# First block of a streaming encoder step: scaling out of PSUM, another place for the fourth tile, fills inside the turns' banks, a pinned order

## The chip, the cores and the metric

The kernel runs on one core of one Trainium2 chip. The core has five engines, each with a queue of its own that is worked off in order: TensorE (PE in the profile, its weight loads PEld), VectorE (DVE), ScalarE (ACT), GpSimd (POOL) and SyncE (SP), which here only issues DMA transfers. They meet through semaphores. SBUF is the working memory; PSUM, eight banks of 128 x 512 fp32, is what PE writes into. The metric is the device time of one launch in microseconds (us), lower is better; several runs are given by their median.

## The reference

One layer of an encoder trunk on 2048 prompt frames and 32 sample frames of 1024 features:

```
hn   = rmsnorm(h, g_mix)
proj = hn @ w_in                       # six parts of 512 columns: h, b, c, za, v, zb
yA   = b * conv3(c * h) * silu(za)     # causal convolution of width 3
yB   = poolmix(v) * silu(zb)           # trailing means of 2/4/8/16 frames, a map per group
h    = h + concat(yA, yB) @ w_out
h    = h + (p @ w_ple) * sigmoid(rmsnorm(h, g_ple) @ w_ple_gate)
y    = rmsnorm(h, g_final)
```

Beside y, the last rows of the convolution's and the pooling's inputs are returned. All is fp32. `rmsnorm` divides a row by the root of its mean square and multiplies it by a vector g along the features.

## The kernel before

Products are made in split form: a factor is cast to a short high part on ACT (line 78), the rest is a low part, got by a subtraction on DVE (line 79), and three products (high by high, high by low, low by high) give one in fp32. The helper `split` issues both; `put` (line 349) does it into a tile's two halves.

The 2080 frames are five blocks of 416. The first two blocks are one group, and its first unit (128 columns of each of the six parts) is done plainly, part after part; the other units use a scheme with seven products for eight. This change lies in what comes before and in that first unit, the first 76 us or so.

Block 0 is fetched as three tiles of 128 frames and a fourth with the last 32 frames of block 0 and the last 32 of block 1 (`ahead0`, `short0`, lines 610 and 611). For each tile ACT sums squares (line 89), POOL makes the mean and, by a power of -1/2, the factor of the row (lines 70 and 74), DVE scales the tile by that factor and by g in two halves of 512 features (`normal`, line 405), PE turns each half into a PSUM bank by four transposes (`turn`, line 412), and `put` splits the bank into `B0`. The vector g reaches all 128 rows through a product with a row of ones into two banks (line 376); DVE copies them to `g_bc` in SBUF (line 377).

PSUM has two rings: `bank` hands out six banks, `tbank` two. A ring hands out a bank once everything that reads its last content is over. Eight turns go through the six; the two of the fourth tile take the banks of the first tile's two. A further bank of the small ring, `idle`, takes transposes of the identity matrix whose result nobody reads, issued by `keep_busy` between the turns (line 615): 8 ahead of the first, then 1, 1, 1, 12, 1, 1, 3 and 2 after the turns.

Then three weights (zb, v, c) are split in halves (`weights`, line 520), and the unit begins with the high-by-high products of the three parts (`upper_parts`, line 585, `zb_first`, `v_first`, `c_first`, 8 products each, line 582). Their low parts follow, and between them PE turns block 1 (`second_block`, line 640: the fourth tile's 32 frames first, then its three tiles), turns a few vectors into a small-ring bank (`vectors`, line 692, `pv`) and goes on with the products of block 1 (`project`, line 570, whose products are on line 565) and the pooling's map (`mix`, line 755, `pm`).

What order an engine gets is decided before the launch by a planner, which goes by the order of the program and by estimated durations. `tc.keep_in_program_order(ins)` pins an instruction: those so marked keep their order among themselves on their engine. Before the change, the fills, the turns, the scalings and the frames' casts of the first block are pinned; the weights' casts, the products of `project` and `mix` aren't.

Of the kernel before, what the change touches and what calls it, by code (L numbers as in the profile page):

```python
# [12 lines left out]
ALU = mybir.AluOpType  # L13
PSUM = bass.MemoryType.PSUM

P = 128
D = 1024
# [7 lines left out]
NB = 416  # L25
GROUPS = [[0, 1], [2, 3], [4]]
NT = SEQ // P + 1
NH = D // 2
KH = KC // 2
# [6 lines left out]
def trunk(ctx, tc, x_p, x_s, c_conv, c_pool, p_p, p_s, g_mix, w_in, conv_w, conv_b, pool_w,  # L36
          pool_scale, w_out, g_ple, w_gate, w_ple, g_fin, y_p, y_s, sc_p, sp_p, sc_s, sp_s):
    nc = tc.nc
# [14 lines left out]
    def bank(name):  # L53
        return ps_m.tile([P, 512], F32, tag="mm", name=name)

    def tbank(name):
        return ps_t.tile([P, 512], F32, tag="tr", name=name)

    ident = const.tile([P, P], F32, name="ident")
# [17 lines left out]
    def split(hi, lo, src, eng=nc.vector):  # L77
        ins = nc.scalar.copy(hi, src)  # L78
        eng.tensor_tensor(lo, src, hi.bitcast(F32), op=ALU.subtract)
        return ins  # L80
# [3 lines left out]
    g_bc = const.tile([P, D], F32, name="g_bc")  # L84
# [223 lines left out]
    def ring4(t, name):  # L308
        return t.tile([P, D], F32, tag="t", name=name)
# [21 lines left out]
    with ExitStack() as s1:  # L331
# [14 lines left out]
        def wtile(name):  # L346
            return wr.tile([P, KH, 2, P], F32R, tag="w", name=name)

        def put(piece, src):

            return split(piece[:, :, 0], piece[:, :, 1], src)

        def ftile(name):
            return wk.tile([P, KH, P], F32, tag="f", bufs=4, name=name)
# [15 lines left out]
        nc.sync.dma_start(gm_row, g_mix)  # L370
        ones = ftile("ones").rearrange("p k n -> p (k n)")[:1, :P]
        nc.vector.memset(ones, 1.0)
        for half in range(2):
            cs = slice(half * NH, half * NH + NH)
            pg = tbank(f"gm_{half}")
            nc.tensor.matmul(pg, ones, gm_row[:, cs], start=True, stop=True)
            nc.vector.tensor_copy(g_bc[:, cs], pg)


        hn = {}  # L380
# [21 lines left out]
        def x_tile(name, rows, squares=junk):  # L402
            return x_stat(x_load(name, rows), squares=squares)

        def normal(x, later=False, cs=slice(0, D)):
            xt, n, r = x
            ins = nc.vector.scalar_tensor_tensor(xt[:n, cs], xt[:n, cs], r[:n], g_bc[:n, cs], op0=ALU.mult,
                                                 op1=ALU.mult)
            if later:
                tc.keep_in_program_order(ins)  # L410

        def turn(x, half, name, get=tbank, later=False):
            xt, n, _ = x
            pt = get(name)
            for k in range(KH):
                kk = half * KH + k
                ins = nc.tensor.transpose(pt[:, k * P:k * P + n], xt[:n, kk * P:(kk + 1) * P], ident[:n, :n])
                if later:
                    tc.keep_in_program_order(ins)
            return pt.rearrange("p (k t) -> p k t", k=KH)[:, :, :n]  # L420
# [91 lines left out]
        def raw_weight(kind, j, name, ring=raw_ring):  # L512
            t = ring(f"raw_{name}")
            col = cols[kind] * WA + j * P
            nc.sync.dma_start(t, w_in[:, col:col + P].rearrange("(k p) n -> p k n", p=P))
            return t
# [3 lines left out]
        def weights(kind, j, name):  # L520

            if first_w:
                return first_w.pop(0)
            raw = raw_weight(kind, j, name, lambda name: raw_of.pop(kind) if kind in raw_of else raw_ring(name))
            out = []
            for half in range(2):
                out.append(wtile(f"w_{name}_{half}"))
                put(out[-1], raw[:, half * KH:half * KH + KH])
            return out

        def pair_weights(gi, ka, kb, j, name, ring, s_ring):
# [26 lines left out]

            return make

        def half_product(ps, lhs, b, start, stop=True):

            for k in range(KH):
                for q, (x, y) in enumerate(((0, 0), (0, 1), (1, 0))):
                    nc.tensor.matmul(ps[:, :NB], lhs[:, k, x], b[:, k, y], start=start and k + q == 0,  # L565
                                     stop=stop and k == KH - 1 and q == 2, skip_group_check=True)

        begun = {}

        def project(ps, w, tb, between=None):  # L570
            x = hn[tb]
            for half in range(2):
                half_product(ps, w[half], x[half], half == 0, half == 1)
                if between and not half:
                    between()

# [8 lines left out]
        def upper_parts(kind, w, tb):  # L585

            ps = bank(f"{kind}_first")
            for half in range(2):
                part_of(ps, w, tb, half, 0, 0, start=half == 0)
            begun[kind] = ps  # L590
# [12 lines left out]
        B0 = {}  # L603
# [6 lines left out]
        ahead0 = [x_tile(f"0_{c}", [x_rows(0, c)], in_raw(kind)) for c, kind in enumerate(raw_of)]  # L610
        short0 = x_tile("0_3", [x_rows(0, 3), x_rows(1, 3)])
        B0.update(six(0))
        idle = tbank("idle")

        def keep_busy(n):

            for _ in range(n):
                tc.keep_in_program_order(nc.tensor.transpose(idle[:, :P], ident, ident))

        keep_busy(8)  # L620
        for x in (*ahead0, short0):
            for half in range(2):
                normal(x, True, slice(half * NH, half * NH + NH))
        for c, x in enumerate([*ahead0, short0]):
            n = P if c < 3 else DEC
            for half, q in enumerate(("11", "21")):
                ins = put(B0[q][:, :, :, c * P:c * P + n], turn(x, half, f"pt0_{c}_{half}", bank, True)[:, :, :n])
                tc.keep_in_program_order(ins)
                keep_busy(((1, 1), (1, 12), (1, 1), (3, 2))[c][half])
        hn[0] = B0["11"], B0["21"]  # L630
        ahead1 = []
        made = []
# [7 lines left out]
        def second_block():  # L640

            spans = [(c, slice(c * P, min(NB, c * P + P))) for c in range(4)]
            xs = [(x_stat(x, True), slice(0, P)) for x in ahead1]
            for x, _ in xs:
                normal(x, True)
            xs.append((short0, slice(DEC, 2 * DEC)))
            yield
            both = {}
            for c, cs in [spans[3], *spans[:3]]:
                x, ts = xs[c]  # L650
                n = ts.stop - ts.start
                both[c] = [x[0][:, half * NH:half * NH + KH * n].rearrange("p (k t) -> p k t", k=KH)
                           for half in range(2)]
                for half, q in enumerate(("12", "22")):
                    pt = turn(x, half, f"pt1_{c}_{half}", bank, later=True)[:, :, ts]
                    put(B0[q][:, :, :, cs], pt)
                    nc.scalar.copy(both[c][half], pt)
                yield
            op = lambda o, a, b, op=ALU.subtract: nc.vector.tensor_tensor(o, a, b, op=op)
            for c, cs in spans:  # L660
                p12, p22 = both[c]
                n = cs.stop - cs.start
                t1, t3, t2, t4 = (ftile(f"f{t}_1_{c}")[:, :, :n] for t in range(4))
                part = lambda q, h: B0[q][:, :, h, cs].bitcast(F32)
                op(t1, p12, part("11", 0))
                op(t3, p22, p12)
                op(t1, t1, part("11", 1))
                op(t2, p22, t1)
                put(B0["T2"][:, :, :, cs], t2)
# [12 lines left out]
        pw = one.tile([P, 2, 4, P], F32R, name="pw")  # L682
# [27 lines left out]
        class Unit:  # L710
# [44 lines left out]
            def mix(self, b):  # L755

                pp, j = self.cols(self.pooled.rearrange("p h n -> p (h n)"), b), self.j
                pq = self.pooled[:, 1, b * NB:b * NB + NB]
                pm = tbank(f"pm_{self.tag}_{b}")
                nc.tensor.matmul(pm[:, :NB], pw[:, 0, j], pp, start=True, stop=False)  # L760
                nc.tensor.matmul(pm[:, :NB], pw[:, 0, j], pq, start=False, stop=False)
                nc.tensor.matmul(pm[:, :NB], pw[:, 1, j], pp, start=False, stop=True)
                z = self.cols(self.zs, b)
                nc.vector.scalar_tensor_tensor(z, pm[:, :NB], pscale(j), z, op0=ALU.mult, op1=ALU.mult)
                self.store(4 + j, b, self.zs)
# [451 lines left out]
    with ExitStack() as s2:  # L1217
# [112 lines left out]
        for i in range(0, NT - 1, 2):  # L1330
            with tc.issue_after(loaded[-1].ins):
                x = [load_rows(xh, "x", i + b, x_p) for b in range(2)] if i else [first_x, second_x]
# [4 lines left out]
            if last:  # L1337
                n = tiles[NT - 1][1]
# [6 lines left out]
            if last:  # L1345
                x = load_rows(xh, "x", NT - 1, x_p, x_s)
# [27 lines left out]
        _, run = embed(rest_e, wp, ring)  # L1374
# [6 lines left out]
        for k in range(KH):  # L1381
            raw = [ring4(xh, f"wg_r{k}_{i}") for i in range(2)]
# [265 lines left out]
        n = tiles[NT - 1][1]  # L1648
# [62 lines left out]
```

## Time and profile before

| | |
|---|---|
| time, median of 3 runs | 921.82 us (920.5 to 921.92) |
| the profiled execution's own time | 921.55 us |
| its span, first to last instruction | 919.8 us |
| PE busy | 907.4 us (99%) |
| DVE, ACT, POOL busy | 723.6, 478.9, 153.6 us |
| DMA | 186.37 MB, mean 203 GB/s |

A row of the profile gives a start and a duration in us from the span's start, the engine, the line of the kernel (L407 is line 407), the operation, what it writes and reads with buffer numbers left out, the shape and, after x, how many were merged into the row. In brackets stands the idle time in front of it and what ended that. PE's durations contain a tail in which the next matmul already runs, so the pace of a run of matmuls is read from the starts. The chain of waits is followed back from the last instruction, at each step to what released it.

### The profile page before, as it was taken

How to read it: one execution, taken by the hardware profiler on the slowest of the kernel's cores; microseconds unless marked ns; L12 is line 12 of the kernel's file. 1: busy time of each engine (PE TensorE's matmuls, PEld its weight loads, DVE VectorE, ACT ScalarE, POOL GpSimd, SP SyncE). 2: the span in 40 equal slices, each digit the busy share in tenths (PEclk: the TensorE clock that was granted, in tenths of full speed). 3: DMA queues.
4: the chain of work that ended last, by engine and by line, in shares of the span. 5: the costliest groups of instructions: out<-in, count | busy, mean ns of one | idle time of the engine just before them, and what ended most of it. 6: DMA issues, size and time to landing. Idle time of an engine off the chain costs nothing.

```text
span 919.8 us, 13006 instructions
## 1 busy us (share of the span) xinstructions
PE 907.4 (99%) x4515; PEld 821.9 (89%) x4515; DVE 723.6 (79%) x1235; ACT 478.9 (52%) x883; POOL 153.6 (17%) x271
## 2 busy tenths in 40 slices
PE   8999999999999999999999999999999999999996
PEld 7999999999999999999999987888877868878885
DVE  6996989999488989785778679665554798888875
ACT  7744565554345555443545446344334875465555
POOL 4111322212001111000000011111111002323333
PEclk9999999999999999999999999999999999999999
DMA  8255595769935555457765359756775885799892
GB/s 261 79 156 151 162 274 157 210 201 314 414 114 162 181 160 187 118 178 264 203 177 170 125 192 295 254 190 184 252 216 170 307 263 146 185 222 241 205 264 101
DMA packets 140734, 186.37 MB, mean 203 GB/s; under 512 B 12060, under 2 KB 111260, under 8 KB 139389
## 3 DMA queue, kind: packets, MB, share of 16 engines
q1 hardware_dynamic: 120237, 126.33, 45.1%
q0 software_dynamic: 17696, 53.71, 20.0%
q10 hardware_dynamic: 2736, 5.51, 1.8%
q8 instruction: 35, 0.57, 0.3%
q14 instruction: 30, 0.25, 0.1%
HBM read 128.93 MB, written 56.56 MB: 202 GB/s over the span
## 4 chain that ended last, share of the span: by engine, by line
PE 89%; DVE 4%; DMA 3%; ACT 1%; issue 1%; SPq 0%; POOL 0%; DVEq 0%; ACTq 0%; POOLq 0%
PE x_o L168 9%; PE x_zbv L565 7%; PE x_ch L565 7%; PE x_zab L565 7%; PE x_g L168 6%; PE e L103 5%; PE z_o L168 4%; PE z_zbv L565 3%; PE z_ch L565 3%; PE z_zab L565 3%; PE b L565 3%; PE za L565 3%; PE h L565 3%; PE z_g L168 3%; PE v L565 2%; PE c L565 2%
## 5 line engine op out<-in xcount | busy, mean ns | idle before, releaser
L103 PE MATMUL e<-wq,pps 128*128 128x512 f32 (+1 forms) x156 | 38.9, 399 | 0.2 <-ACT pps L78 0.2
L78 ACT CAST y_S<-y_fS 128x512 fp32r<-128x512 f32 x32 | 19.3, 621 | 38.0 <-PE x_o L168 20.0
L168 PE MATMUL x_o<-wo_b,y_S 128*128 128x512 f32 x128 | 35.7, 390 | 0.0
L168 PE MATMUL x_g<-wg_b,g_S 128*128 128x512 f32 x128 | 35.7, 389 | 0.0
L565 PE MATMUL z_zbv<-B,w_zbv_S 128*128 128x416 f32 x168 | 34.2, 352 | 0.0
L565 PE MATMUL x_ch<-B,w_ch_S 128*128 128x416 f32 x168 | 34.1, 351 | 0.0
L565 PE MATMUL z_zab<-B,w_zab_S 128*128 128x416 f32 x168 | 34.1, 351 | 0.0
L565 PE MATMUL x_zab<-B,w_zab_S 128*128 128x416 f32 x168 | 34.0, 351 | 0.0
L565 PE MATMUL x_zbv<-B,w_zbv_S 128*128 128x416 f32 x168 | 34.0, 351 | 0.0
L565 PE MATMUL z_ch<-B,w_ch_S 128*128 128x416 f32 x168 | 34.0, 351 | 0.0
L1438 POOL DMA_DIRECT2D e<-h_d x28 | 24.9, 908 | 53.8 <-DVE e L1435 46.3
L103 PEld LDWEIGHTS e<-wq,pps 128*128 128x128 f32 (+1 forms) x156 | 27.4, 182 | 6.9 <-ACT pps L78 0.5
L70 POOL TENSOR_SCALAR ms_x<-ssq_x 128x1 f32<-128x1 f32 (+2 forms) x18 | 12.3, 682 | 122.7 <-ACT junk L89 118.5
L565 PEld LDWEIGHTS x_zab<-B,w_zab_S 128*128 128x128 f32 x168 | 31.3, 188 | 0.4
L565 PEld LDWEIGHTS x_zbv<-B,w_zbv_S 128*128 128x128 f32 x168 | 31.4, 188 | 0.3
L565 PEld LDWEIGHTS z_ch<-B,w_ch_S 128*128 128x128 f32 x168 | 31.4, 188 | 0.3
L565 PEld LDWEIGHTS z_zab<-B,w_zab_S 128*128 128x128 f32 x168 | 31.3, 188 | 0.3
L565 PEld LDWEIGHTS x_ch<-B,w_ch_S 128*128 128x128 f32 x168 | 31.3, 188 | 0.3
L565 PEld LDWEIGHTS z_zbv<-B,w_zbv_S 128*128 128x128 f32 x168 | 31.3, 188 | 0.4
L78 ACT CAST y<-y 128x512 fp32r<-128x512 f32 x24 | 14.8, 618 | 30.8 <-PE z_o L168 12.8
L168 PEld LDWEIGHTS x_o<-wo_b,y_S 128*128 128x128 f32 x128 | 24.0, 188 | 5.1 <-ACT c_o L1241 0.3
L168 PEld LDWEIGHTS x_g<-wg_b,g_S 128*128 128x128 f32 x128 | 24.0, 188 | 4.9
(607 smaller groups left out, 2656.2 us busy)
## 6 DMA issues: line engine op xcount, KB each, us to landing
y<-y_d SPq DMA_DIRECT2D x16, 512.0 KB, 6.2
x<-in_x_prompt_dram SPq DMA_DIRECT2D x16, 512.0 KB, 5.7
h_d<-x SPq DMA_DIRECT2D x16, 512.0 KB, 2.6
hn<-h_d SPq DMA_DIRECT2D x61, 128.0 KB, 6.6
xt<-in_x_prompt_dram SPq DMA_DIRECT2D x15, 512.0 KB, 5.3
e<-e_d SPq DMA_DIRECT2D x15, 512.0 KB, 6.1
e<-h_d POOLq DMA_DIRECT2D x28, 256.0 KB, 7.0
out_dram<-e POOLq DMA_DIRECT2D x13, 512.0 KB, 4.1
```

Source lines behind the costliest of these rows:

```text
L70: nc.gpsimd.tensor_scalar(ms[:n], ssq[:n], scalar1=1.0 / D, scalar2=EPS, op0=ALU.mult, op1=ALU.add)
L78: ins = nc.scalar.copy(hi, src)
L103: nc.tensor.matmul(ps[:n], pps[:, a, k, :n], wp[k][b][:, cs], start=k + q == 0, stop=k == 1 and q == 2)
L168: nc.tensor.matmul(ps[:n], lhs[:, k, a, :n], w[b][:, k], start=start and k + q == 0, stop=k == KH - 1 and q == 2, skip_group_check=True)
L565: nc.tensor.matmul(ps[:, :NB], lhs[:, k, x], b[:, k, y], start=start and k + q == 0, stop=stop and k == KH - 1 and q == 2, skip_group_chec ...
L1438: nc.gpsimd.dma_start(ee, h_d[r:r + P, at[1] * NH:at[1] * NH + NH], accum_op=ALU.add)
```

## The change

- `g_ps` keeps the two PSUM banks with g, and the new `normal_half` scales the four tiles of block 0 with g out of PSUM. The copies to `g_bc` stay, since the later scalings read them. The two banks are the whole small ring, and they stay in use until the last of the eight scalings.
- The fourth tile's turns take their banks from the small ring, both in block 0 and in block 1; the `idle` bank and `keep_busy` are gone.
- The unread transposes are written into the bank of the turn that follows them, by the argument `fill` of `turn`: 6, 1, 1, 1, 4, 1, 0, 0 ahead of the eight turns, and 4 in the bank of `zb_first` ahead of its products.
- Pinned in addition: the casts of the three first weights, the products of `project` for block 1, and the first product of `mix` in the first unit.

```diff
+        g_ps = []
         for half in range(2):
             pg = tbank(f"gm_{half}")
             nc.tensor.matmul(pg, ones, gm_row[:, cs], start=True, stop=True)
             nc.vector.tensor_copy(g_bc[:, cs], pg)
+            g_ps.append(pg)
...
-        def normal(x, later=False, cs=slice(0, D)):
+        def normal(x, later=False):
...
+        def normal_half(x, half):
+            xt, n, r = x
+            cs = slice(half * NH, half * NH + NH)
+            tc.keep_in_program_order(
+                nc.vector.scalar_tensor_tensor(xt[:n, cs], xt[:n, cs], r[:n], g_ps[half][:n], op0=ALU.mult, op1=ALU.mult))
+
-        def turn(x, half, name, get=tbank, later=False):
+        def turn(x, half, name, get=tbank, later=False, fill=0):
             xt, n, _ = x
             pt = get(name)
+            for _ in range(fill):
+                tc.keep_in_program_order(nc.tensor.transpose(pt[:, :P], ident, ident))
...
-                put(out[-1], raw[:, half * KH:half * KH + KH])
+                ins = put(out[-1], raw[:, half * KH:half * KH + KH])
+                if name[:5] == "first":
+                    tc.keep_in_program_order(ins)
...
-                half_product(ps, w[half], x[half], half == 0, half == 1)
+                half_product(ps, w[half], x[half], half == 0, half == 1, tb == 1)
...
             ps = bank(f"{kind}_first")
+            for _ in range(4 if kind == "zb" else 0):
+                tc.keep_in_program_order(nc.tensor.transpose(ps[:, :P], ident, ident))
...
-        idle = tbank("idle")
-        def keep_busy(n):
-            for _ in range(n):
-                tc.keep_in_program_order(nc.tensor.transpose(idle[:, :P], ident, ident))
-        keep_busy(8)
+        FILL = (6, 1), (1, 1), (4, 1), (0, 0)
         for x in (*ahead0, short0):
             for half in range(2):
-                normal(x, True, slice(half * NH, half * NH + NH))
+                normal_half(x, half)
         for c, x in enumerate([*ahead0, short0]):
             n = P if c < 3 else DEC
             for half, q in enumerate(("11", "21")):
-                ins = put(B0[q][:, :, :, c * P:c * P + n], turn(x, half, f"pt0_{c}_{half}", bank, True)[:, :, :n])
+                ins = put(B0[q][:, :, :, c * P:c * P + n], turn(x, half, f"pt0_{c}_{half}", bank if c < 3 else tbank, True, FILL[c][half])[:, :, :n])
                 tc.keep_in_program_order(ins)
-                keep_busy(((1, 1), (1, 12), (1, 1), (3, 2))[c][half])
...
-                    pt = turn(x, half, f"pt1_{c}_{half}", bank, later=True)[:, :, ts]
+                    pt = turn(x, half, f"pt1_{c}_{half}", tbank if c == 3 else bank, later=True)[:, :, ts]
...
-                nc.tensor.matmul(pm[:, :NB], pw[:, 0, j], pp, start=True, stop=False)
+                ins = nc.tensor.matmul(pm[:, :NB], pw[:, 0, j], pp, start=True, stop=False)
+                if self.gi + j == 0:
+                    tc.keep_in_program_order(ins)
```

More of the change, by code (lines that the diff above doesn't have):

```diff
@@ L403, in x_tile @@
             return x_stat(x_load(name, rows), squares=squares)
-        def normal(x, later=False, cs=slice(0, D)):
+        def normal(x, later=False):
             xt, n, r = x
-            ins = nc.vector.scalar_tensor_tensor(xt[:n, cs], xt[:n, cs], r[:n], g_bc[:n, cs], op0=ALU.mult,
-                                                 op1=ALU.mult)
+            ins = nc.vector.scalar_tensor_tensor(xt[:n], xt[:n], r[:n], g_bc[:n], op0=ALU.mult, op1=ALU.mult)
             if later:
                 tc.keep_in_program_order(ins)
-        def turn(x, half, name, get=tbank, later=False):
+        def normal_half(x, half):
[4 more added lines that the diff above has]
+        def turn(x, half, name, get=tbank, later=False, fill=0):
             xt, n, _ = x
             pt = get(name)
+            for _ in range(fill):
+                tc.keep_in_program_order(nc.tensor.transpose(pt[:, :P], ident, ident))
             for k in range(KH):
@@ L559, in pair_weights, with half_product @@
             return make
-        def half_product(ps, lhs, b, start, stop=True):
+        def half_product(ps, lhs, b, start, stop=True, later=False):
             for k in range(KH):
                 for q, (x, y) in enumerate(((0, 0), (0, 1), (1, 0))):
-                    nc.tensor.matmul(ps[:, :NB], lhs[:, k, x], b[:, k, y], start=start and k + q == 0,
-                                     stop=stop and k == KH - 1 and q == 2, skip_group_check=True)
+                    ins = nc.tensor.matmul(ps[:, :NB], lhs[:, k, x], b[:, k, y], start=start and k + q == 0,
+                                           stop=stop and k == KH - 1 and q == 2, skip_group_check=True)
+                    if later:
+                        tc.keep_in_program_order(ins)
         begun = {}
@@ L759, in mix @@
                 pm = tbank(f"pm_{self.tag}_{b}")
-                nc.tensor.matmul(pm[:, :NB], pw[:, 0, j], pp, start=True, stop=False)
+                ins = nc.tensor.matmul(pm[:, :NB], pw[:, 0, j], pp, start=True, stop=False)
+                if self.gi + j == 0:
+                    tc.keep_in_program_order(ins)
                 nc.tensor.matmul(pm[:, :NB], pw[:, 0, j], pq, start=False, stop=False)
```

## The prediction

> **What bounds the kernel now.** I read the page's totals first, then what TensorE (PE) waited for, then the chain of waits over the first 60 us, then each engine's rows in order of time there.
>
> ```profile
> span 919.8 us, 13006 instructions
> PE 907.4 (99%) x4515; PEld 821.9 (89%) x4515; DVE 723.6 (79%) x1235; ACT 478.9 (52%) x883; POOL 153.6 (17%) x271
> ...
> PE pt L417 <- ACT xt L657: 0.8, 1, 0.8
> PE x_g L168 <- ACT c_g L1424: 0.4, 1, 0.4
> PE pt L417 <- DVE B L79: 0.4, 1, 0.4
> ```
>
> PE is busy for 907.4 of 919.8 us. Its waits for another engine (last column: the longest, us) are tiny, and the two on `pt` both lie in the first block, where this change works. So time is won only by letting PE's unbroken run begin earlier, or by removing those two waits. The profiled execution took 921.55 us; the median of the runs is 921.82, 0.27 above it.
>
> The chain of waits in the first block, where each line is start, length, work:
>
> ```profile
> 8.91 1.15 ACT junk L89 x2
> ...
> 10.58 0.76 POOL ms_x L70
> ...
> 11.41 0.95 POOL rstd_x L74
> ...
> 12.39 1.41 DVE xt L407 x2
> 13.79 0.61 DVE B L79
> ```
>
> This is the fourth frame tile (32 + 32 rows): its sum of squares on ACT, mean and root on POOL, the two scaling halves on DVE, then a subtraction on DVE that frees the PSUM bank its turns wait for. The sum was there at 8.91 + 1.15 = 10.06, yet POOL began 0.5 us later, because the third tile's root had held it. Why was POOL late?
>
> ```profile
> 7.07 0.55 POOL L70 TENSOR_SCALAR ms_x<-ssq_x 128x1 f32<-128x1 f32 x1 [0.46 <-ACT raw_firstv L89]
> 7.70 0.94 POOL L74 TENSOR_TENSOR rstd_x<-ms_x,nhalf 128x1 f32<-128x1 f32 x1
> 8.85 0.63 POOL L70 TENSOR_SCALAR ms_x<-ssq_x 128x1 f32<-128x1 f32 x1 [0.21 <-ACT raw_firstc L89]
> 9.56 0.94 POOL L74 TENSOR_TENSOR rstd_x<-ms_x,nhalf 128x1 f32<-128x1 f32 x1
> ...
> 6.83 1.40 DVE L407 SCALAR_TENSOR_TENSOR xt<-xt,rstd_x,g_bc 128x512 f32<-128x512 f32 x2
> 8.68 1.41 DVE L407 SCALAR_TENSOR_TENSOR xt<-xt,rstd_x,g_bc 128x512 f32<-128x512 f32 x2 [0.45 <-POOL rstd_x L74]
> 10.53 1.42 DVE L407 SCALAR_TENSOR_TENSOR xt<-xt,rstd_x,g_bc 128x512 f32<-128x512 f32 x2 [0.44 <-POOL rstd_x L74]
> ```
>
> POOL's one-column operations take 0.55 to 0.94 us while DVE scales. Late in the kernel the same two operations stand beside DVE work of two kinds:
>
> ```profile
> 846.25 0.65 DVE L1614 TENSOR_TENSOR g_fS<-hn,g_fS 128x512 f32<-128x512 f32 x1
> ...
> 847.42 0.68 DVE L1432 TENSOR_TENSOR c_g<-x_g,c_g 128x512 f32<-128x512 f32 x1
> ...
> 846.28 1.05 POOL L74 TENSOR_TENSOR rstd_f<-ms_f,nhalf 128x1 f32<-128x1 f32 x1
> 847.42 0.19 POOL L70 TENSOR_SCALAR ms_f<-ssq_f 128x1 f32<-128x1 f32 x1
> 847.69 0.55 POOL L74 TENSOR_TENSOR rstd_f<-ms_f,nhalf 128x1 f32<-128x1 f32 x1
> ```
>
> Beside a DVE operation with both inputs in SBUF the root took 1.05; beside one with an input in PSUM (`x_g` is a bank) mean and root took 0.19 and 0.55. POOL is held up by DVE's second SBUF input. The Trainium skill states the same cause ("GPSIMD Engine Reference", section Key points: contention with DVE instructions that have two SBUF inputs); by that rule, too, the change frees POOL, and the trace agrees with 0.55 against 1.05.
>
> **The change, part by part.**
>
> *Scaling reads g from PSUM.* Eight scalings keep their count. Price of a PSUM input on DVE, with a per-row scalar in both rows:
>
> ```profile
> 44.48 0.65 DVE L764 SCALAR_TENSOR_TENSOR zs<-pm,vec,zs 128x416 f32<-128x416 f32 x1
> ...
> 55.60 0.64 DVE L809 SCALAR_TENSOR_TENSOR c_s<-U,vec,c_s 128x416 f32<-128x416 f32 x1
> ```
>
> 0.01 each, at most 0.08 for eight: taken as nothing. The copies into `g_bc` stay (later scalings use it), so the first scaling may still stand behind the second copy: no gain there. What POOL gains: mean 0.19, a gap of 0.08 (7.07 + 0.55 to 7.70), root 0.55, together 0.82. Tile 1: 7.07 + 0.82 = 7.9, then DVE is the limit, free at 6.83 + 1.40 = 8.2. Tile 2: its sum still releases POOL at 8.85, so its root is there at 9.7 and its scaling runs 9.7 to 11.1 (before: 10.53). Tile 3: sum at 10.06, root at about 10.95, scaling 11.1 to 12.5 instead of 12.39 to 13.80. DVE is 1.3 us earlier, and its queue of subtractions behind follows at once.
>
> *Fourth tile into g's banks.* Its turns no longer need a bank that the first subtraction frees, so the wait of 0.4 goes. The two banks are freed by the very scalings that make the turns' data, so nothing new is waited for. What is late next is the data, at 12.5.
>
> *Fills.* Unread turns go from 8+1+1+1+12+1+1+3+2 = 30 to 6+1+1+1+4+1+4 = 18; they occupy PE only, and have to be seen against PE's pace and ACT's casts:
>
> ```profile
> 6.11 1.97 PE L618 MATMUL idle<-ident 128*128 128x128 f32 x8
> ...
> 10.01 1.06 PE L417 MATMUL pt<-ident,xt 128*128 128x128 f32 x4
> 11.07 0.60 PE L417 MATMUL pt<-ident,xt 128*128 128x128 f32 x4
> 11.51 1.47 PE L618 MATMUL idle<-ident 128*128 128x128 f32 x12
> ...
> 15.91 1.77 PE L582 MATMUL zb_first<-B,w_firstzb 128*128 128x416 f32 x8
> ...
> 9.97 2.33 ACT L78 CAST B<-pt 128x512 fp32r<-128x512 f32 x4
> 13.46 1.13 ACT L78 CAST B<-pt 128x512 fp32r<-128x512 f32 x2 [1.16 <-PE pt L417]
> ...
> 15.11 0.62 ACT L78 CAST w_firstzb<-raw_firstzb 128x512 fp32r<-128x512 f32 x1
> ...
> 15.82 0.27 ACT L78 CAST B<-pt 128x128 fp32r<-128x128 f32 x1
> ```
>
> A turn costs PE 0.21 until about 11.0 and 0.11 after it (four plus a fill between 10.01 and 11.07; four between 11.07 and 11.51). First turn: six fills end at 6.11 + 1.3 = 7.4, the first half's data at 6.83 + 0.70 = 7.5, so 7.6. Sixteen turns and three fills then run to 11.4, four fills to 11.8, the third tile and its fill to 12.8, the fourth tile's two short groups (no more than the 0.44 of a full one) to 13.6, the four fills in `zb_first` to 14.0. Today the twelve fills end only at 12.8, and ACT idles 1.16 for it.
>
> *Casts pinned.* ACT is the later of the two: free at 10.06, six casts at 2.33/4 = 0.58 end at 13.5, two short ones at 13.9. The first weight cast was slipped in ahead of the last short one (15.11 before 15.82); pinned, it stands behind, 0.6 on the path and hidden by nothing: 14.5. `zb_first` begins at about 14.55 instead of 15.91: -1.35. The next casts (0.57 apart) stay ahead of products that take 0.8 per half. The weight loads must also be there earlier; today no cast waits for them, and a late one would cost up to the 1.35.
>
> *Second block.* The rows around the wait of 0.8:
>
> ```profile
> 29.03 0.28 DVE L79 TENSOR_TENSOR B<-pt,B 128x128 fp32r<-128x128 f32 x1
> ...
> 33.15 0.68 DVE L79 TENSOR_TENSOR B<-pt,B 128x512 fp32r<-128x512 f32 x1
> ...
> 29.34 0.27 ACT L657 COPY xt<-pt 128x128 f32<-128x128 f32 x1 [0.24 <-DVE B L79]
> ...
> 29.66 0.66 PE L417 MATMUL pt<-ident,xt 128*128 128x128 f32 x4 [0.80 <-ACT xt L657]
> ...
> 30.19 1.76 PE L582 MATMUL c_first<-B,w_firstc 128*128 128x416 f32 x8
> ...
> 34.17 4.69 PE L565 MATMUL zb<-B,w_firstzb 128*128 128x416 f32 x24
> ```
>
> The last turn in front of `c_first` waits for the bank of the fourth tile's first turn, freed by the copy at 29.34 + 0.27. With that tile in the two small-ring banks, the turn has a bank at once; but `pv` (the vectors' turn behind it) takes a small-ring bank, so it now waits for the same copy. Only the four turns move into the wait, 0.44. Then `zb` needs the subtraction that ends at 33.15 + 0.68 = 33.83 and starts at 34.17 today, so no more than 0.34 is kept. Bounds: nothing, and the whole 0.8.
>
> *Products and `pm` pinned.* PE already runs them in that order: nothing. The cover is that their data are ready; if a pinned one is late, the next product can't pass it.
>
> **Sum:** 1.35 + 0.35 = 1.7 us off 921.55 gives 919.85, 0.21% under the median.
>
> **The rivals.**
>
> *The clock (slower).* Fewer fills could leave PE at its early pace when the 24 products of the three upper parts run. At half pace each costs its 4.69/24 = 0.195 once more, 4.7 in all: 921.55 - 1.7 + 4.7 = 924.55. It is slower by over 0.2% (1.84 us, about what a measurement of this kernel tells from no change) once 19 of the 24 are slow. Against it: PE has no gap over 0.2 us between 7.6 and 13.6 by my rows. The Trainium skill ("TensorE: Matmul & The Clock Gate", Part 1) states that the clock halves when idle and comes back after a busy window of about 3.4 us, whose phase is free; the change of pace near 11.0 agrees. By that rule a missed window holds only nine such products, an estimate of 1.7 lost, and the result is no change.
>
> *POOL isn't freed.* If the scaling still holds POOL up, DVE ends at 13.80 as before. `zb_first` starts 0.7 earlier, but DVE's subtractions, the second block's scalings and the copy at 29.34 don't move, so only the second block's 0.35 to 0.45 is left: 921.15. The row at 847.69 speaks against it.
>
> *The order behind.* The planner orders all that isn't pinned by its own costs; a moved start can give DVE and ACT another order in the second block or among the seven-product units. DVE has hardly a gap there (25.39 us busy of 25.80, the third figure of this row of a table by stage):
>
> ```profile
> 34.20:60.00 25.80, 25.80 (x138) 25.54 (x137) 25.39 (x45) 15.94 (x29) 1.92 (x2) 1.00 0.26 78
> ```
>
> So one operation put ahead of one that PE needs costs 0.68 (the row at 33.15). Five such (3.4) turn the gain into a loss over 0.2%; two or three leave no change: 922 to 925. PE's few waits today show an order that fits; whether it stays can't be read from this profile.
>
> *More than the sum.* The second block's queues keep the whole 0.8 and the tail of the scalings comes better: 919.0.
>
> **How the numbers follow.** Main line 0.50 (919.1 to 920.6, as its border is near 0.2%: 0.36 faster, 0.14 same); clock 0.08 (slower); POOL not freed 0.10 (same); order behind 0.22 (0.15 slower, 0.07 same); more 0.10 (faster). Faster 0.46, same 0.31, slower 0.23. The range goes from 918.6 (below the better case) to 924.0 (most of the order's).
>
> **What would show it.** Right: POOL's means and roots of tiles 1 to 3 at about 0.19 and 0.55; the fourth tile's scaling over by 12.5; no wait of PE on `pt` for DVE; the first `zb_first` product near 14.55 at a pace of 0.195; `pv` waiting for the copy out of the fourth tile's turn; `zb` near 32.5; every later stage shifted by about 1.7. Wrong: roots still at 0.94; products at twice 0.195; ACT waiting for a weight load; or a wait of PE behind 34 us that isn't in the list above.

## The result, and the profile after

The changed kernel takes 920.67 us (median of 22 runs, 918.85 to 923.21), the kernel before 922.11 (22 runs, 920.5 to 924.28). The ratio, taken over all runs and not from the two medians (which lie 1.44 apart), is 0.9982, with a 95% interval of 0.9976 to 0.9988: faster by 1.66 us, 1.1 to 2.2. A second set of runs gave 0.9983 (0.9975 to 0.9992). So the gain of 1.7 us that was forecast came, though not where it was forecast: of the 2.1 us between the first pair of profiles, 0.7 lie in the first 35 us, and the rest behind 560 us.

The totals of the profile after, and PE's waits (engine, line, tile, what released it; us in total, times, longest):

```profile
span 917.7 us, 12980 instructions
PE 905.8 (99%) x4503; PEld 820.6 (89%) x4503; DVE 724.1 (79%) x1235; ACT 478.3 (52%) x883; POOL 151.4 (17%) x271
...
PE pv L701 <- ACT xt L664: 0.8, 1, 0.8
PE x_zab L576 <- DVE U L925: 0.3, 1, 0.3
PE e L103 <- ACT pps L78: 0.2, 1, 0.2
PE pt L426 <- DVE xt L417: 0.2, 1, 0.2
```

The profiled execution took 919.83 us. The wait of the fourth tile's turn for a bank (on `pt`, for DVE's subtraction `B`) is gone; what is left on `pt` is a wait for DVE's scaling itself, 0.2 here and up to 1.6 in further profiles with a later third tile. The wait on `pt` for ACT has moved to `pv` at its full 0.8. The waits on `x_g` are gone too, far behind anything that was changed.

The rows of POOL, DVE, ACT and PE in the first block of the same profile, in order of time on each engine:

```profile
7.07 0.19 POOL L70 TENSOR_SCALAR ms_x<-ssq_x 128x1 f32<-128x1 f32 x1 [0.41 <-ACT raw_firstv L89]
7.34 0.55 POOL L74 TENSOR_TENSOR rstd_x<-ms_x,nhalf 128x1 f32<-128x1 f32 x1
10.21 0.19 POOL L70 TENSOR_SCALAR ms_x<-ssq_x 128x1 f32<-128x1 f32 x1 [2.31 <-ACT raw_firstc L89]
...
11.07 2.75 DVE L417 SCALAR_TENSOR_TENSOR xt<-xt,rstd_x,gm 128x512 f32<-128x512 f32 x4 [1.51 <-POOL rstd_x L74]
13.74 4.06 DVE L79 TENSOR_TENSOR B<-pt,B 128x512 fp32r<-128x512 f32 x8
...
8.97 1.06 ACT L89 ACTIVATE raw_firstc<-xt 128x1024 bf16<-128x1024 f32 x1 [1.99 <-DMA xt<-in_x_prompt_dram]
10.34 1.06 ACT L89 ACTIVATE junk<-xt 64x1024 bf16<-64x1024 f32 x1 [0.21 <-DMA xt<-in_x_prompt_dram]
...
15.25 1.78 PE L595 MATMUL zb_first<-B,w_firstzb 128*128 128x416 f32 x8
...
29.42 0.32 PE L701 MATMUL pv<-ident,rows 112*128 112x112 f32 x1 [0.79 <-ACT xt L664]
33.48 2.86 PE L576 MATMUL zb<-B,w_firstzb 128*128 128x416 f32 x14
```

POOL's mean and root take 0.19 and 0.55 beside the scalings, as forecast. But the third tile's sum starts at 8.97 here, held for 1.99 by its transfer. In the profile of before it was:

```profile
7.62 1.06 ACT L89 ACTIVATE raw_firstc<-xt 128x1024 bf16<-128x1024 f32 x1 [0.63 <-DMA xt<-in_x_prompt_dram]
```

The input came 1.35 us later, and `zb` still started 0.69 earlier (33.48 against 34.17). Two single profiles can't be compared as they stand. Further ones of both kernels were needed first.

### The profile page after: what moved, and what is told of

It is laid out like the page before. It is cut to its first block, busy times and chain, and to the rows that moved or that the text cites. A ratio compares the mean times of both kernels' runs of the same rounds, so it can differ in the third digit from the quotient of the medians.

```text
span 917.7 us, 12980 instructions
## 1 busy us (share of the span) xinstructions
PE 905.8 (99%) x4503; PEld 820.6 (89%) x4503; DVE 724.1 (79%) x1235; ACT 478.3 (52%) x883; POOL 151.4 (17%) x271
## 4 chain that ended last, share of the span: by engine, by line
PE 96%; DVE 1%; ACT 1%; DMA 1%; issue 0%; SPq 0%; POOL 0%; ACTq 0%; DVEq 0%; POOLq 0%
PE x_o L168 9%; PE x_g L168 9%; PE x_zbv L576 7%; PE x_ch L576 7%; PE x_zab L576 7%; PE e L103 5%; PE z_g L168 5%; PE z_o L168 4%; PE z_zbv L576 3%; PE z_ch L576 3%; PE z_zab L576 3%; PE b L576 3%; PE za L576 3%; PE h L576 3%; PE zb L576 2%; PE v L576 2%
## 5 line engine op out<-in xcount | busy, mean ns | idle before, releaser
L1245 DVE TENSOR_TENSOR c_o<-x_o,x 128x512 f32<-128x512 f32 x14 | 9.7, 690 | 23.9 <-PE x_o L168 23.9
```

Source lines behind the costliest of these rows:

```text
L1245: add = lambda o, a, b: nc.vector.tensor_tensor(o, a, b, op=ALU.add)
```

## The experiments

Two theories were put against each other. By the first (that of the prediction's sum), the end of the DVE chain of the first block moves PE's run as a whole: POOL freed, the fourth tile's wait gone, the cast order and the second block's bank each add their term. By the second, `zb` and all behind it hang on DVE's queue, and an earlier `zb_first` only makes the wait in front of `zb` longer. The clock, a rival of the prediction, was tried as well; another rival, the order behind, was read from the traces.

### Both kernels again, unchanged

> The kernel before, unchanged, one more profiled execution, to see how the arrival of the third frame tile (the start of ScalarE's third sum of squares: 7.62 in the first profile of before, 8.97 in that of after, 7.51 to 9.59 in the four experiments) varies without any change. Theory (arrival varies by itself, and the change acts behind it): with an early arrival (7.6) the first product of zb_first is near 15.9, with a late one (9.0 to 9.6) near 17. Rival (the change moves the arrival): it is near 7.6 here each time.

> As the run before it: the kernel before once more. From the end of the fourth tile's sum to the first product of zb_first 5.5 to 5.9 us by the theory, whatever the arrival.

> The changed kernel, unchanged, one more profiled execution. Theory: with an early arrival the first product of zb_first is near 14.5 and zb near 32.3, as in the run with twelve fills; with a late one near 15.3 and 33.5, as in the first profile of after. From the end of the fourth tile's sum to the first product 3.8 us when late, 4.5 when early (ScalarE's casts are then the limit).

> As the run before it: the changed kernel once more. Behind zb every start is shifted against the kernel before by the same amount up to 540 us; what differs beyond that is chance and not the change.

Starts in us, read from the rows of each profile: the third tile's sum, the end of the fourth tile's sum, DVE's first subtraction, `zb_first`, `zb`. The last column tells how much later PE's instructions stand than in the first profile after, compared one by one (median), between 100 and 490 us and at 910 us.

| profile | third sum | fourth sum ends | subtraction | zb_first | zb | shift, middle / end |
|---|---|---|---|---|---|---|
| before | 7.62 | 10.06 | 13.72 | 15.91 | 34.17 | 0.62 / 2.06 |
| before, second | 8.69 | 11.53 | 14.23 | 16.42 | 34.67 | 1.1 / 2.30 |
| before, third | 9.19 | 11.85 | 14.47 | 16.65 | 34.91 | 1.35 / 1.28 |
| after | 8.97 | 11.49 | 13.74 | 15.25 | 33.48 | 0 / 0 |
| after, second | 9.02 | 11.82 | 14.07 | 15.58 | 34.06 | 0.6 / 0.41 |
| after, third | 9.43 | 11.89 | 14.16 | 15.64 | 34.16 | 0.68 / 0.77 |

The sum of the third tile, which waits for its transfer, begins anywhere between 7.62 and 9.19 us in one and the same program. The third profiles of both kernels have the same end of the fourth sum (11.85 and 11.89) and can be compared. Before, third profile (POOL, DVE, PE):

```profile
11.94 0.18 POOL L70 TENSOR_SCALAR ms_x<-ssq_x 64x1 f32<-64x1 f32 x1 [0.69 <-ACT junk L89]
12.20 0.90 POOL L74 TENSOR_TENSOR rstd_x<-ms_x,nhalf 64x1 f32<-64x1 f32 x1
...
13.14 1.41 DVE L407 SCALAR_TENSOR_TENSOR xt<-xt,rstd_x,g_bc 64x512 f32<-64x512 f32 x2 [0.44 <-POOL rstd_x L74]
14.47 3.67 DVE L79 TENSOR_TENSOR B<-pt,B 128x512 fp32r<-128x512 f32 x6
...
16.65 1.78 PE L582 MATMUL zb_first<-B,w_firstzb 128*128 128x416 f32 x8
34.91 0.35 PE L565 MATMUL zb<-B,w_firstzb 128*128 128x416 f32 x1
```

After, third profile:

```profile
12.23 0.54 POOL L74 TENSOR_TENSOR rstd_x<-ms_x,nhalf 64x1 f32<-64x1 f32 x1
...
11.52 2.71 DVE L417 SCALAR_TENSOR_TENSOR xt<-xt,rstd_x,gm 128x512 f32<-128x512 f32 x4 [2.14 <-POOL rstd_x L74]
14.16 4.06 DVE L79 TENSOR_TENSOR B<-pt,B 128x512 fp32r<-128x512 f32 x8
...
15.64 1.77 PE L595 MATMUL zb_first<-B,w_firstzb 128*128 128x416 f32 x8
30.10 0.31 PE L701 MATMUL pv<-ident,rows 112*128 112x112 f32 x1 [1.13 <-ACT xt L664]
34.16 1.16 PE L576 MATMUL zb<-B,w_firstzb 128*128 128x416 f32 x5
```

With a late third tile POOL is held up only once, at the last root (0.90 against 0.54), and DVE's gap of 0.44 behind it goes: the first subtraction is 0.31 earlier, not 1.3. `zb_first` gains 1.01, and `zb` 0.75. The distance from the first subtraction to `zb` is 20.44 to 20.45 in the three profiles before, and 19.74 to 20.00 in the three after. It doesn't follow `zb_first`: of the 1.01, `zb` keeps 0.31 from the subtraction and 0.44 from the shorter distance, and the wait ahead of it grows from 0.85 (on `pt`) to 1.13 (on `pv`). From the start of `pv` to `zb` PE takes 4.05 to 4.07 in the profiles after, so what releases `pv` sets `zb`: ACT's copy, which stands behind DVE's subtraction for the fourth tile of block 1. (The first profile after has 19.74 because DVE's first scaling of block 1 waits 0.45 for POOL there, and 0.72 in the two others.) Counted from the end of the fourth sum, the second profiles give a gain of 0.45 for the subtraction and 0.90 for `zb`. From there to `zb_first` it took 5.85, 4.89 and 4.80 in the profiles before, so the 5.5 to 5.9 that were expected for any arrival were missed with a late tile; in the profiles after it took 3.76 to 3.77, as expected.

### g read from SBUF again

```diff
- nc.vector.scalar_tensor_tensor(xt[:n, cs], xt[:n, cs], r[:n], g_ps[half][:n], ...)
+ nc.vector.scalar_tensor_tensor(xt[:n, cs], xt[:n, cs], r[:n], g_bc[:n, cs], ...)
```

> The changed kernel, but the eight scalings read g from the SBUF copy again. All else, the order on every engine included, is the same. Theory (a PSUM input on VectorE leaves GpSimd free): the means and roots of tiles 1 to 3 go back from 0.19 and 0.55 us to about 0.55 to 0.75 and 0.94, the gap from the end of the fourth tile's sum to its first scaling grows by some 0.5 to 0.7 us, and the kernel loses about 1.3 of its 1.7 us: ratio to the kernel before near 0.9995. Rival (the freed GpSimd is worth nothing, the gain comes from banks and fills): the ratio stays near 0.998.

```profile
11.44 0.56 POOL L70 TENSOR_SCALAR ms_x<-ssq_x 64x1 f32<-64x1 f32 x1 [0.27 <-ACT junk L89]
12.09 0.94 POOL L74 TENSOR_TENSOR rstd_x<-ms_x,nhalf 64x1 f32<-64x1 f32 x1
...
13.05 1.40 DVE L417 SCALAR_TENSOR_TENSOR xt<-xt,rstd_x,g_bc 64x512 f32<-64x512 f32 x2 [0.44 <-POOL rstd_x L74]
14.39 4.06 DVE L79 TENSOR_TENSOR B<-pt,B 128x512 fp32r<-128x512 f32 x8
...
34.38 0.80 PE L576 MATMUL zb<-B,w_firstzb 128*128 128x416 f32 x3
```

Those rows are of this kernel's profile. Mean and root are back at 0.56 and 0.94, and the gap of 0.44 with them. The fourth sum ended at 11.36, so the subtraction stands 3.03 behind it (2.25 to 2.27 in the three profiles after) and `zb` 23.02 (21.99 to 22.27). Against these profiles the operand in PSUM alone is worth 0.75 to 1.0 us of `zb`'s start. But the spacing of the arrivals differs: here the fourth sum ends 2.25 behind the start of the third, there 2.46 to 2.80. The kernel with block 1's old bank (below), with g in PSUM and the same 2.25, has its subtraction 2.48 behind, which makes it 0.55. Time: 0.9993 of before (0.9983 to 1.0003). From the first subtraction to `zb` it takes 19.99, as in the changed kernel: the second block's part isn't touched by it.

### The fourth tile's bank, in block 0 and in block 1 alone

```diff
 # block 0
- turn(x, half, f"pt0_{c}_{half}", bank if c < 3 else tbank, True, FILL[c][half])
+ turn(x, half, f"pt0_{c}_{half}", bank, True, FILL[c][half])
 # block 1, the other kernel
- turn(x, half, f"pt1_{c}_{half}", tbank if c == 3 else bank, later=True)
+ turn(x, half, f"pt1_{c}_{half}", bank, later=True)
```

> The changed kernel, but the fourth tile's turns of block 0 take a bank of the large ring again. Theory: they wait for the first subtraction, which stands behind the last scaling on VectorE, so the first product of zb_first comes some 0.6 us later and the ratio rises to about 0.9988; a wait of TensorE for VectorE on pt of about 0.4 to 0.6 is back. Rival (ScalarE's casts set the time, the bank doesn't): no wait that matters, ratio near 0.998. The planner also orders a few VectorE operations of block 1 differently here, which this run can't keep apart.

> The changed kernel, but the fourth tile's turns in block 1 take banks of the large ring again. Theory (what moved is only the last four turns ahead of the wait): the wait is back on pt, in front of four turns instead of pv, and from the first subtraction of block 0 to zb the distance goes back from 20.0 to 20.44 us; ratio some 0.0005 higher, too little to be told by the times alone. Rival (the place of the wait doesn't matter, because zb waits for VectorE's subtraction): the distance stays at 20.0.

Rows of the kernel with block 0's bank put back:

```profile
14.83 1.05 PE L426 MATMUL pt<-ident,xt 64*128 64x64 f32 x8 [1.25 <-DVE B L79]
...
16.75 1.78 PE L595 MATMUL zb_first<-B,w_firstzb 128*128 128x416 f32 x8
34.10 1.22 PE L576 MATMUL zb<-B,w_firstzb 128*128 128x416 f32 x5
```

The wait for the subtraction is back, at 1.25. `zb_first` stands 5.16 behind the fourth sum's end (11.59) instead of 3.76, so it lost 1.40. `zb` stands 22.51 behind it, only some 0.25 more than after, and that is what the first subtraction lost by the spacing of the arrivals (2.50 behind instead of 2.25): from it to `zb` it takes 20.00, as in the changed kernel. The wait in front of `pv` is no longer there, it has been used up. This tells the theories apart: as long as DVE sets `zb`, an earlier `zb_first`, here by 1.1 us and more, is worth nothing to `zb`. Time: 0.9998 (0.9986 to 1.0009), though twelve runs from 919.08 to 924.27 settle little, and the planner gave a few operations of DVE and ACT in the second block another order here, as it did for the next kernel.

Rows of the kernel with block 1's bank put back:

```profile
29.87 0.66 PE L426 MATMUL pt<-ident,xt 128*128 128x128 f32 x4 [1.58 <-ACT xt L664]
34.37 4.69 PE L576 MATMUL zb<-B,w_firstzb 128*128 128x416 f32 x24
```

The wait is on `pt` again, 1.58 long, and the first subtraction (13.93) to `zb` takes 20.44 as before. So this part is worth 0.44, where 0.34 was forecast. Time: 0.9997 (0.9985 to 1.0008); this profile also lost 2.2 us far behind, 1.8 of them behind a late transfer (below).

### Twelve fills, and none

```diff
- FILL = (6, 1), (1, 1), (4, 1), (0, 0)
+ FILL = (6, 1), (1, 1), (12, 1), (0, 0)   # one kernel
+ FILL = (0, 0), (0, 0), (0, 0), (0, 0)    # the other, without the four in zb_first too
```

> The changed kernel with 12 unread turns ahead of the third tile's first turn instead of 4, as many as the kernel before had there. Theory (they delay the third tile): eight more at 0.11 us hold TensorE 0.9 us, ScalarE's casts wait for it, and zb_first starts 0.5 to 0.9 later: ratio near 0.9988. Rival (the arrival of the third and fourth tile sets the time, TensorE has room): ratio near 0.998.

> The changed kernel with no unread turns at all. Theory of the clock: TensorE is then not busy enough to leave its early pace, and the 24 products of the upper parts run in part at 0.39 instead of 0.195 us: 1.7 to 4.7 us slower, ratio 1.000 to 1.003. Rival (the real turns are enough): the pace changes at about the same time, the products run at 0.195, ratio 0.998 or a little less.

Rows of the kernel with twelve:

```profile
7.51 1.06 ACT L89 ACTIVATE raw_firstc<-xt 128x1024 bf16<-128x1024 f32 x1 [0.61 <-DMA xt<-in_x_prompt_dram]
...
14.44 1.78 PE L595 MATMUL zb_first<-B,w_firstzb 128*128 128x416 f32 x8 [0.30 <-ACT w_firstzb L78]
32.23 3.06 PE L576 MATMUL zb<-B,w_firstzb 128*128 128x416 f32 x15
```

Here the third tile came as early as in the profile that the prediction started from, and the starts are those that it gave: 14.44 against 14.55, 32.23 against 32.5. PE waits for a cast of ACT, so the eight more fills were hidden, and leaving them out gains nothing at this arrival. Time: 0.9994 (0.9985 to 1.0003); this profile lost 0.8 us again behind 560 us.

Rows of the kernel without fills:

```profile
16.01 3.14 PE L595 MATMUL zb_first<-B,w_firstzb 128*128 128x416 f32 x8 [0.87 <-ACT w_firstzb L78]
18.95 2.71 PE L595 MATMUL v_first<-B,w_firstv 128*128 128x416 f32 x8
21.50 1.67 PE L595 MATMUL c_first<-B,w_firstc 128*128 128x416 f32 x8
```

And two stretches of its table by time (stretch; length, busy time and count of PE, PEld, DVE, ACT, POOL; granted clock; DMA share; GB/s):

```profile
16.00:21.50 5.50, 5.49 (x17) 5.27 (x17) 5.50 (x12) 5.44 (x10) 1.81 (x1) 0.52 0.66 229
21.50:34.00 12.50, 12.48 (x79) 11.76 (x79) 9.67 (x17) 6.42 (x17) 4.75 (x6) 1.00 0.60 164
```

The eight products of `zb_first` took 2.94 (16.01 to 18.95) instead of 1.62 (15.25 to 16.87 in the profile after), those of `v_first` 2.55 instead of 1.51, at a granted clock of 0.52; the same table of the changed kernel has 1.00 from 13.3 us on. That is 2.4 us on PE: the rival of the clock is real, and the 18 fills that are left keep clear of it in all four profiles of the changed kernel, though PE waits up to 1.44 us for the third tile in one of them. Against what was expected, PE without fills doesn't stay at its early pace, it falls back: turns stand 0.21 apart until 10.8 us and 0.11 from 12.5 on, and the granted clock is 0.50 from 14.40 to 21.23 us, after a stretch of 3.40 us in which PE was busy for 1.95, with no wait over 1.31. The Trainium skill ("TensorE: Matmul & The Clock Gate", Part 1) states that the clock follows a free-running window of about 3.4 us. This trace agrees: the 6.83 us at half clock are two such windows.

Time: 0.9993 (0.9980 to 1.0005), an interval that holds the lower end of what was expected and reaches its rival. The twelve runs lie in two groups, six from 918.97 to 920.00 and six from 921.68 to 923.89, and the one with the profile (922.30) is in the second. So the 2.4 us need not be lost in every run; what the clock did in the others no trace shows.

This kernel, the one with twelve fills, the one with g from SBUF and the one with block 0's old bank were timed in one set of runs, without the changed kernel. All four came to 0.9993 to 0.9998, even that with twelve fills, whose profile shows nothing lost in the first 34 us. So their ratios, set beside the 0.998 of other sets, price no part of the change; only their traces do.

### DVE's low parts given to GpSimd

If DVE's queue sets `zb`, three subtractions less in it, two of them ahead of what `pv` waits for, should help.

```diff
- split(pw[:, 0], pw[:, 1], pw_raw)
+ split(pw[:, 0], pw[:, 1], pw_raw, nc.gpsimd)     # and both halves of w_h
```

> The changed kernel, but three low parts (pw and both halves of w_h in the first unit) are made by GpSimd instead of VectorE. In the changed kernel two of them (0.60 apart) stand on VectorE ahead of the subtraction that the copy for pv waits for. Theory (behind zb_first it is VectorE's queue, not TensorE, that sets when zb starts: from its first subtraction of block 0 to zb 20.0 us in both repeats of the changed kernel, 20.44 in all three profiles of the kernel before): that distance shrinks by 0.6 to 1.2 us, to 18.8 to 19.4, the wait of about 1 us on pv goes, and the kernel gains up to as much, ratio near 0.997. Rival (TensorE's own run sets it): the distance and the ratio stay. What can spoil it: GpSimd gets SBUF only in VectorE's gaps, so the low parts may come late; then pm (needed about 43) or h (about 48) waits and the kernel is slower.

```profile
28.05 2.24 POOL L79 TENSOR_TENSOR w_h<-raw_h,w_h 128x512 fp32r<-128x512 f32 x1
...
26.88 2.29 DVE L409 SCALAR_TENSOR_TENSOR xt<-xt,rstd_x,g_bc 128x1024 f32<-128x1024 f32 x1 [0.72 <-POOL rstd_x L74]
29.10 1.65 DVE L791 TENSOR_TENSOR win<-V 128x416 f32<-128x416 f32 x1
...
31.30 0.31 PE L701 MATMUL pv<-ident,rows 112*128 112x112 f32 x1 [1.97 <-ACT xt L664]
```

It got slower: 1.0010 (1.0001 to 1.0020) of before. The rows of its profile show that the hindrance goes both ways: beside GpSimd's two subtractions a scaling of 1.28 took 2.29, and an addition of 0.58 took 1.65. The wait in front of `pv` grew to 1.97 and the way from the first subtraction to `zb` from 20.0 to 20.90. The expected gain was wrong in sign. The mechanism behind it (DVE's queue sets `zb`) is borne out from the other side.

### g in PSUM for the second block too

```diff
+ g_two = [tbank(f"g_two_{half}") for half in range(2)]      # copied from g_bc by ACT
- for x, _ in xs: normal(x, True)
+ for x, _ in xs:
+     for half in range(2): normal_half(x, half, g_two)
```

> The changed kernel, and in addition the three scalings of block 1 read g out of PSUM, as halves: ScalarE copies g back into the two small-ring banks behind its three sums of squares, and the banks are free again before the turns of block 1. The planner moves one low part of w_h on VectorE behind the turns' subtractions with it. Theory (VectorE's queue sets when zb starts, and GpSimd, held up by the scalings' second SBUF input, makes gaps of 0.72 us in that queue): the means and roots of block 1 run under the scalings, the two gaps of 0.72 go, and from the first subtraction of block 0 to zb the distance falls from 20.0 to about 18.2 to 18.6 us, where TensorE's own run takes over; the wait on pv goes; 1.0 to 1.5 us faster than the changed kernel, ratio to the kernel before near 0.997. Rival (the copies on ScalarE come too late for the first scaling, or the turns of the fourth tile wait for the banks): no gain, ratio near 0.998.

> The changed kernel again, timed beside the run above on the same chip: ratio to the kernel before 0.998 to 0.999, and in the profile from the fourth tile's sum to zb_first 3.76 us if the third tile arrives late, about 4.5 if early.

Rows of the kernel with g in PSUM twice:

```profile
21.01 4.04 DVE L417 SCALAR_TENSOR_TENSOR xt<-xt,rstd_x,g_two 128x512 f32<-128x512 f32 x6 [0.49 <-POOL rstd_x L74]
27.75 0.32 PE L705 MATMUL pv<-ident,rows 112*128 112x112 f32 x1
31.82 4.69 PE L576 MATMUL zb<-B,w_firstzb 128*128 128x416 f32 x24
57.05 7.26 PE L576 MATMUL za<-B,w_za 128*128 128x416 f32 x37 [0.90 <-DVE w_za L79]
```

Six scalings in 4.04 us without a gap, no wait in front of `pv`, and `zb` 18.97 behind the first subtraction instead of 20.0: DVE sets `zb`, shown by making DVE faster. But the time is 0.9989 (0.9980 to 0.9998) of before, not to be told from the 0.9983 (0.9975 to 0.9992) of the changed kernel on the same chip. In this profile 1.2 us of the gain are given back by `za`, which waits 0.90 for a low part from DVE. At the start of the output projection, from 563 to 568 us, PE loses another 1.5 against the changed kernel's profile; there DVE waits 1.86 for the transfer of `y` (0.27 in the other), so that is an arrival, as below. No kernel here was measured faster than the changed one.

### Where the rest of the gain lies

The shift in the table above is flat up to 490 us in every profile. Behind that, two of three profiles of before lose another 1.4 and 1.2 us, around 568, 816 and 865 us, and the third none; the three profiles after and that of the timed repeat lose none. At 816 us the profile of before has, on POOL, ACT and PE:

```profile
799.66 0.89 POOL L1438 DMA_DIRECT2D e<-h_d  x1 [0.84 <-DVE e L1435]
...
807.66 1.06 ACT L89 ACTIVATE junk<-e 128x1024 bf16<-128x1024 f32 x1 [1.05 <-DMA e<-h_d]
...
818.39 0.50 PE L168 MATMUL x_g<-wg_a,g_S 128*128 128x512 f32 x1 [0.44 <-ACT c_g L1424]
```

and the third profile of before, the same two steps:

```profile
799.87 0.89 POOL L1438 DMA_DIRECT2D e<-h_d  x1 [0.85 <-DVE e L1435]
...
806.71 1.06 ACT L89 ACTIVATE junk<-e 128x1024 bf16<-128x1024 f32 x1
```

A reload of h, which adds onto what is there, is issued at 799.66 and 799.87; ACT's sum of squares waits for it until 807.66 in one, and starts without a wait at 806.71 in the other. From issue to use 8.00 us pass in the one, 6.84 in the other, 7.36 in the profile after (798.60 to 805.96), and 8.91 in the kernel with block 1's old bank (800.18 to 809.09), where PE then lost 1.47 on `x_g`. The chain on ACT and DVE behind that sum stands 0.95 later in the first, up to the copy that `x_g` waits for (817.76 against 816.81). At the two other places DVE waits for a transfer: ahead of 568 us 0.51 and 0.55 for `y` in the two profiles that lose, not at all in the third and at most 0.27 in those after; at 866 us 2.25 and 2.63 for `hn`, 1.03 in the third, at most 0.21 in those after (up to 1.5 in variants of the changed kernel). It is one program with one order, so the late losses are arrivals of transfers.

On average over three profiles of each kernel, before lies 1.5 us behind after at 910 us, 0.6 of it at 100 to 490 us (1.3 and 0.4 with the timed repeat). So of the gain of 1.66, only the part at the front is traced to the change. Whether the kernel before meets late transfers more often, or three profiles happened to show it so, stays open.

## Why the prediction was right or wrong

**The forecast, 919.85 (faster).** Measured 920.67, a gain of 1.66 for the 1.7 forecast; the 0.8 between them is mostly the start: the sum was made against 921.55, and the median of before over 22 runs is 922.11. At 0.18% the gain lies just under the 0.2% that the prediction took as its border, though its interval is clear of no gain. That the sum met the measured gain is in part luck, as the points show.

**"POOL is held up by DVE's second SBUF input."** Right, in every profile after: 0.19 and 0.55; put back, 0.52 to 0.56 and 0.94. The rival "POOL isn't freed" is out.

**"DVE is 1.3 us earlier."** This is the step that failed as a number. It took the arrival of the third tile in one profile (7.62) for a property of the kernel. At that arrival it holds, as far as the kernel with twelve fills shows it: the first subtraction comes 2.43 behind the fourth sum (12.24 less 9.81) against 3.66 before, 1.23 less, and `zb` 22.42 against 24.11, 1.69 less. With the tile at 8.7 to 9.4 DVE gains 0.31 to 0.45, and `zb` 0.75 to 0.90.

**"`zb_first` begins at about 14.55 instead of 15.91", and the sum 1.35 + 0.35.** Right in size at the early arrival (14.44), but added up along the wrong chain. The sum let PE's run move as a whole, although the prediction's own rival "POOL isn't freed" has it that an earlier `zb_first` is worth nothing while DVE doesn't move. `zb` follows DVE's queue: put block 0's bank back, and `zb_first` loses 1.40 while `zb` loses 0.25. So `zb` gains DVE's shift and 0.44 from block 1's bank: 1.23 and 0.46 at the early arrival, 0.31 and 0.44 at the late one. At the early arrival DVE moves by about as much as PE, and both chains give the same number.

**The fourth tile's wait of 0.4 and the first weight cast's 0.6.** Present as told: the wait for the bank was 0.4, 0.9 and 0.7 in the three profiles before and none after, and the cast is now behind the last short one. Both bear on `zb_first`; that the bank moves little of `zb` is shown by putting it back, for the cast no run shows it.

**"Only the four turns move into the wait", at most 0.34 kept.** The wait on `pv` came, at 0.8 to 1.1; kept were 0.44, all four turns, both from before to after and with the bank put back. The bound of 0.34 was too tight: in the first profile after `zb` starts at 33.48, ahead of the end of the subtraction that was to hold it (33.57). The "more than the sum" rival, the whole 0.8, did not come.

**The clock (0.08).** Its mechanism was shown without fills, at 2.4 us rather than 4.7 (the estimate for one window that the prediction gave beside it, 1.7, was nearer), and is absent with 18. The premise against it, no gap of PE over 0.2 us until 13.6, held in none of the further profiles (0.30, 1.20 and 1.44), and the clock stayed full all the same. **The order behind (0.22).** PE's order behind the fills is the same in both kernels, and PE has no new wait there. **"Products and `pm` pinned: nothing."** PE has these products in the same order before (not pinned) and after (pinned), so nothing is right as far as the traces show; no run leaves out the pins alone.

**"Every later stage shifted by about 1.7."** Wrong: 0.6 to 0.7 in the first pair of profiles up to 490 us. The other 1.4 of that pair's 2.06 are waits for transfers at 568 us and later, which no step of the prediction had.

## What to carry to other kernels

Before a chain at the start of a kernel is summed, take two or three profiles of the same program: where a transfer's arrival moves by more than the gain in question, give the gain for both arrivals. Measure a chain from the event that the change can't move (the end of the fourth sum here), and check which engine's distance to the next long run stays constant; that engine's earlier start counts, and another's turns into a wait. An operand that is in PSUM anyway was read from there at no price (four scalings in 2.71 us, two in 1.41 from SBUF), and it freed GpSimd, which is worth something only where GpSimd is on the path.

## What was not expected of the hardware

- A 128 x 1024 load at the start of the kernel comes between 7.5 and 9.9 us in one program or its close variants (the third tile's sum starts at 7.51 in one kernel, at 9.91 in the timed repeat of the changed one); a reload in the middle of the run took 8.91 us from issue to use in one profile, and no more than 6.84 in another.
- The hindrance between DVE and GpSimd goes both ways and is large for full tiles: 1.28 became 2.29 and 0.58 became 1.65 on DVE, while GpSimd's own subtraction took 1.28 and 2.24 for the same 128 x 512.
- A one-column mean on POOL, 0.19 us undisturbed, is held behind a whole run of DVE subtractions with two inputs in SBUF, not behind one of them: it took 1.37 to 2.57 us, and in 12 of 14 profiles it ended 0.05 to 0.06 behind the last of them whenever it had begun (21.44 against 21.39 before, 21.79 against 21.74 in the second profile after).
- PE's clock fell to half without a long wait of PE: in the kernel without fills after 3.40 us with no wait over 1.31, while one of 1.44 left it full in the timed repeat of the changed kernel.
